# A hybrid HGRN2 and S5 block on one core: half of the S5 setup ordered behind a weight split, later steps of two heads, and the last head's squares on other engines

## The chip, the core and the metric

The kernel runs on one core of a Trainium2 chip. Its engines work from their own in-order queues: TensorE (PE in the profile; its weight loads are PEld), VectorE (DVE), ScalarE (ACT), GpSimd (POOL) and SyncE (SP), which issues DMAs. Engines wait for one another by semaphores, which the tile framework sets from the data that each instruction reads and writes.

The metric is the time of one execution in microseconds on the device, as the median of several runs. Three runs of the kernel before took 796.67, 797.11 and 803.19 us; the median is 797.11 us. One further execution was profiled: it took 799.9 us, of which the profile shows a span of 797.7 us.

## What is computed

One layer of a decoder trunk for 512 tokens of width 1024, in float32, and a final RMSNorm. Cut to what matters here:

```python
h = rmsnorm(x, g)                       # 512 x 1024
q, f, i, og, u, gate_hg, gate_s5 = split(h @ w_in)
# HGRN2, 4 heads of 128, chunks of 64 tokens
f = lb + (1 - lb) * sigmoid(f);  k = 1 - f;  q = silu(q)
b = cumsum(log(f))                      # within a chunk
scores = causal((q * exp(b - b_ref)) @ (k * exp(b_ref - b)).T)
o = scores @ v + (q * exp(b)) @ S_prev  # S: state carried over chunks
o = o * rsqrt(mean(o * o) + eps) * norm_g * silu(og)
# S5, 32 groups with 64 complex states: x_t = A x_{t-1} + B u_t, y = Re(C x) + D u
g = gelu(y);  s5 = g * sigmoid(g @ glu_w + glu_b)
x = x + (sigmoid(gate_hg) * (o @ w_branch_hg) + sigmoid(gate_s5) * (s5 @ w_branch_s5)) @ w_out
x = x + conv_gated_ffn(rmsnorm(x))      # 1024 -> 2 x 2816 -> 1024
x = x + sigmoid(rmsnorm(x) @ w_ple_gate) * (p @ w_ple_proj)
return rmsnorm(x)
```

## The kernel before

**Products in three parts.** Each large float32 operand is split into a high half in a shorter format (float32r) and a low half, the rest. A product is then three matmuls, high x high, high x low and low x high, summed in PSUM (`mm3`, lines 229 to 235; the matmuls are lines 231, 232 and 233 in the profile). The split itself is one copy on ScalarE and one subtraction on VectorE (`split`, lines 241 to 244; the subtraction is line 244).

**Weights** stream through in chunks of up to 128 x 1024. SyncE loads a chunk into `wst` (two slots), ScalarE makes `whi` (three slots) and VectorE `wlo` (three slots), all in `emit_w`. Chunks 0 to 5 hold the weights for u, the input of S5; chunk 6 holds those of f of head 0, chunk 7 q, chunk 8 og. From chunk 3 on the split stands in a block of high priority.

**The order of work.** PE's instructions run in the order in which the program writes them. The main line is: u (`phase_u`, PSUM tiles `psu`, with head 0's f behind it, `pf`), then as `ORDER` says: the rest of head 0, v (`psv`), head 1, gate 0, head 2, gates 1 and 2, head 3, gates 3 to 7, each a run of `mm3`; then the GLU of S5 (`psg`), the two branch products (`pbh`, `pbs`), w_out, the FFN and the last part. Between the `mm3` of the main line stand the small matmuls of the recurrences. They come from two generators, `hg_side` for each head after the other and `s5_side` for four blocks of S5 groups. A counter, `clock`, is raised by 0.65 with each `mm3` and by what a small matmul is put down for; whenever it passes the time that a generator asked for with `yield WAIT[...]`, the next step of that generator is written. `WAIT["hg"][h]` has five entries, the delays ahead of head h's five steps:

- the elementwise work of the head (lines 485 to 517: sigmoids, log, the scan of line 499, the differences of lines 502 and 504, exponentials, products; its last results are `q`, line 513, and `e`, line 511), then entry 0 ahead of the score matmuls `psc`
- entry 1 ahead of the transposes `pk`, entry 2 ahead of the state products `pu`, entry 3 ahead of the outputs `pso`
- then the square of `pso` on ScalarE (line 569), its high and low half on GpSimd (`osh`, line 572, and `osl`, line 573), and entry 4 ahead of the sum over the head, `pms` (lines 576 and 577), and what makes `yhg` of it (lines 579 to 584)

Head h + 1's generator starts when head h's is through. An S5 block makes tables (`Fr`, `Fi`, `Hr`, `Hi`, lines 723 to 742, on VectorE and GpSimd in turn), then the small matmuls `ps5k`, transposes `ps5t` (copied to `et` by ScalarE, line 764), inputs `ps5v`, and, after a scan on VectorE, outputs `ps5y`. When all four are through, `s5_out` brings the result back by DMA (`yT`), applies GELU (`gf`) and splits it (`gh`, `gl`).

The order on VectorE, ScalarE, GpSimd and in the DMA queues is not written by hand. The framework's scheduler takes, by its own estimate of when things are ready, the most urgent instruction that is ready; what was written earlier is more urgent, and a block of high priority more than the rest.

**The S5 setup** (`s5_setup`, lines 615 to 701) is written behind u and in a block of high priority. It works on VectorE in small steps. The first half makes step angles, sine and cosine, the powers `Ar`, `Ai` and the coefficients `nr`, `ni` (to line 685). The second half (from line 686) makes Bbar from them (`bbr`, `bbi`, copied into `Bbr` and `Bbi`) and the powers `Wr`, `Wi` up to 64 by doubling. The reciprocal root of the first norm (`rstd`, lines 344 to 353) and its spreading over the tokens (`dg`, `psR`, `R`, lines 366 to 369) also stand at high priority; `R` scales u (`uT`, line 409), f, q and og (line 480).

**Lines that the steps below touch**: `WAIT` at line 35; `emit_w` with the split in `do`; `split`; in `hg_side` lines 569 to 577; `s5_setup`; the call in the main program behind `phase_u()` and `hg_setup()`.

Of the kernel before, what the change touches and what calls it, by code (L numbers as in the profile page):

```python
# [8 lines left out]
F32 = mybir.dt.float32  # L9
# [3 lines left out]
ALU = mybir.AluOpType  # L13
# [9 lines left out]
HEADS = 4  # L23
# [11 lines left out]
WAIT = {  # L35
    "r": [16.5, 17.5],
    "hg": [[19.5, 3.5, 4.5, 5, 7],
           [13.5, 3.5, 5.5, 5, 10],
           [18.0, 4, 4, 5.5, 7.5],
           [22.0, 3.5, 4, 9, 6.5]],  # L40
    "s5": [[20, 0, 2, 13, 0],
           [9, 2, 16.5, 12.5, 4.0],
           [7, 1.5, 5.5, 15, 0],
# [70 lines left out]
def hybrid_kernel(ctx: ExitStack, tc: tile.TileContext, a):  # L114
# [67 lines left out]
    def split_w(i):  # L182
        split_w_.pop(i)()

    early = {}

    def w_chunk(i, off):
        n = chunk_size(plan[i])
# [6 lines left out]
    def emit_w(dst=None):  # L195
        i = wstate["next"]
        n = chunk_size(plan[i])
        off = wstate["off"]
        wst = early.pop(i, None)
        if wst is None:  # L200
            wst = wp.tile([P, CW], F32, tag="wst", bufs=2, name=f"wst{i}")
            nc.sync.dma_start(wst[:, :n], w_chunk(i, off))
        if dst:
            whi, wlo = dst
        else:
            whi = wp.tile([P, CW], F32R, tag="whi", bufs=LOOK + 1, name=f"whi{i}")
            wlo = wp.tile([P, CW], F32R, tag="wlo", bufs=LOOK + 1, name=f"wlo{i}")

        def do():
            split(whi[:, :n], wlo[:, :n], wst[:, :n])  # L210

        if i < 3:
            split_w_[i] = do
        else:
            with tc.high_priority():
                do()
        wstate["off"] += P * n
        wstate["next"] += 1
        return whi, wlo
# [21 lines left out]
    def split(hi, lo, src):  # L241

        S.activation(hi, src, AF.Copy)  # L243
        V.tensor_tensor(out=lo, in0=src, in1=hi.bitcast(F32), op=ALU.subtract)  # L244

    def act_pair(name):
        return (ap_.tile([P, KD, T], F32R, tag="ahi", name=name + "h"),
# [236 lines left out]
    def hg_side(h):  # L484
# [84 lines left out]
        S.activation(osq, pso, AF.Square)  # L569
        osh = hgt("e1", h, dt=F32R)  # L570
        osl = hgt("e2", h, dt=F32R)
        G.tensor_scalar(out=osh, in0=osq, scalar1=1.0, scalar2=0.0, op0=ALU.mult, op1=ALU.add)
        G.tensor_tensor(out=osl, in0=osq, in1=osh.bitcast(F32), op=ALU.subtract)
        yield WAIT["hg"][h][4]
        pms = small_ps("pms")
        E.matmul(pms, onesr, osh, start=True, stop=False)
# [38 lines left out]
    def s5_setup():  # L615
# [67 lines left out]
        V.tensor_tensor(out=ni, in0=ni, in1=tq, op=ALU.subtract)  # L683
        V.tensor_tensor(out=nr, in0=nr, in1=den, op=ALU.mult)
        V.tensor_tensor(out=ni, in0=ni, in1=den, op=ALU.mult)
        t1, t2 = tmp2(GP, 16)
        cmul(V, br_, bi_, bc(nr.unsqueeze(2), P, GP, 16), bc(ni.unsqueeze(2), P, GP, 16), bcp[:, 0], bcp[:, 1],
             t1, t2)
# [198 lines left out]
    phase_u()  # L887
    hg_setup()
    with tc.high_priority():
        s5_setup()  # L890
    for b in range(4):
        s5_load(b)
    hg = side(hg_all())
# [309 lines left out]
```

## Time and profile before

| what | before |
|---|---|
| median of three runs | 797.11 us |
| the profiled execution's own time | 799.9 us |
| its span in the profile | 797.7 us |
| PE busy | 781.1 us (98%) |
| VectorE busy | 521.3 us (65%) |
| ScalarE busy | 358.2 us (45%) |
| GpSimd busy | 104.7 us (13%) |
| HBM read, written | 80.72 MB, 4.69 MB |

How to read it: a row of the timeline has the start in the span, the duration, the engine, the line, the operation, the tile written and those read, shapes, and in square brackets how long the engine was idle before it and what it waited for. A row of the table of stretches has the stretch, its length, then for each of PE, PEld, DVE, ACT and POOL the busy time and the number of instructions, then the granted TensorE clock as a share of the full one, the mean share of the DMA engines, and GB/s. A row of the view of waits says who waited for whom, how long in total, how often and how long at most. Matmuls are pipelined: one of 128 x 512 is shown with about 0.39 us, while the next may start 0.23 us after it.

### The profile page before, as it was taken

What the parts mean: (1) busy time and instruction counts of PE and PEld (TensorE: products, weight loads), DVE (VectorE), ACT (ScalarE), POOL (GpSimd) and SP (SyncE); (2) the same over time, 40 slices, a digit from 0 to 9 for tenths busy, and PEclk for the clock granted to TensorE, in tenths of its full rate; (3) what the DMA queues carried; (4) which work ended last, traced back from release to release, by engine and by line L of the source; (5) the groups of instructions that cost most, each with busy time, mean ns of one, the idle gap of its engine ahead of it and who ended that gap; (6) DMA issues with size and microseconds to landing.
All of it is one profiled execution on the core that took longest, in us unless ns stands there. A gap on an engine that the chain in (4) does not pass through costs nothing.

```text
span 797.7 us, 9972 instructions
## 1 busy us (share of the span) xinstructions
PE 781.1 (98%) x3806; PEld 640.8 (80%) x3806; DVE 521.3 (65%) x827; ACT 358.2 (45%) x470; POOL 104.7 (13%) x133
## 2 busy tenths in 40 slices
PE   9899999999999999999999999999999999999996
PEld 7687877878888778888888888888888888888885
DVE  7998885898683676375887666777666234144554
ACT  7335373463753933253443443443443133133565
POOL 2044341341521100032000000000000001011000
PEclk9999998999999999999999999999999999999999
DMA  9472524223353232623223233233222223223411
GB/s 336 162 176 79 134 67 109 81 66 110 93 121 95 67 112 99 211 80 106 84 101 106 83 102 106 82 103 106 85 100 93 80 94 105 89 89 138 160 53 53
DMA packets 27039, 86.10 MB, mean 108 GB/s; under 512 B 4720, under 2 KB 4864, under 8 KB 26992
## 3 DMA queue, kind: packets, MB, share of 16 engines
q1 hardware_dynamic: 22608, 77.58, 29.2%
q0 software_dynamic: 3664, 6.84, 4.3%
q10 hardware_dynamic: 720, 1.05, 0.4%
q8 instruction: 30, 0.49, 0.3%
q14 instruction: 17, 0.14, 0.1%
HBM read 80.72 MB, written 4.69 MB: 107 GB/s over the span
## 4 chain that ended last, share of the span: by engine, by line
PE 82%; DVE 9%; issue 2%; DMA 2%; ACT 2%; POOL 1%; SPq 0%; DVEq 0%; POOLq 0%; ACTq 0%
PE pdn L233 5%; PE pdn L232 5%; PE pdn L231 5%; PE puv L231 5%; PE pug L231 5%; PE puv L233 5%; PE pug L233 5%; PE puv L232 5%; PE pug L232 5%; PE pw L233 2%; PE pw L231 2%; PE pw L232 2%; DVE wlo L244 2%; PE ps5y L172 2%; PE pgh L231 1%
## 5 line engine op out<-in xcount | busy, mean ns | idle before, releaser
L243 ACT ACTIVATE whi<-wst 128x1024 fp32r<-128x1024 f32 (+1 forms) x124 | 128.7, 1038 | 269.2 <-issue 77.2
L244 DVE TENSOR_TENSOR wlo<-wst,whi 128x1024 fp32r<-128x1024 f32 (+1 forms) x124 | 153.4, 1237 | 126.0 <-ACT whi L243 126.0
L233 PE MATMUL pdn<-gh,wlo 128*128 128x512 f32 x176 | 70.2, 399 | 0.0
L231 PE MATMUL pdn<-gh,whi 128*128 128x512 f32 x176 | 69.5, 395 | 0.0
L232 PE MATMUL pdn<-gl,whi 128*128 128x512 f32 x176 | 69.4, 394 | 0.0
L231 PE MATMUL pug<-x1gh,whi 128*128 128x512 f32 x160 | 62.2, 389 | 0.0
L232 PE MATMUL pug<-x1gl,whi 128*128 128x512 f32 x160 | 62.2, 389 | 0.0
L233 PE MATMUL pug<-x1gh,wlo 128*128 128x512 f32 x160 | 62.2, 389 | 0.0
L231 PE MATMUL puv<-x1gh,whi 128*128 128x512 f32 x160 | 62.2, 389 | 0.0
L232 PE MATMUL puv<-x1gl,whi 128*128 128x512 f32 x160 | 62.2, 389 | 0.0
L233 PE MATMUL puv<-x1gh,wlo 128*128 128x512 f32 x160 | 62.2, 389 | 0.0
L946 POOL TENSOR_TENSOR sqs<-sqs,sq 128x512 f32<-128x512 f32 x14 | 23.2, 1659 | 222.7 <-ACT sq L945 218.5
L232 PEld LDWEIGHTS pdn<-gl,whi 128*128 128x128 f32 x176 | 33.1, 188 | 8.3
L233 PEld LDWEIGHTS pdn<-gh,wlo 128*128 128x128 f32 x176 | 33.0, 188 | 7.6
L231 PEld LDWEIGHTS pdn<-gh,whi 128*128 128x128 f32 x176 | 33.1, 188 | 7.6
L984 DVE TENSOR_TENSOR u<-pug,R 128x512 f32<-128x512 f32 x20 | 13.8, 692 | 38.4 <-PE pug L233 38.4
L233 PEld LDWEIGHTS puv<-x1gh,wlo 128*128 128x128 f32 x160 | 30.0, 188 | 6.3
L232 PEld LDWEIGHTS pug<-x1gl,whi 128*128 128x128 f32 x160 | 30.0, 188 | 6.3
L233 PEld LDWEIGHTS pug<-x1gh,wlo 128*128 128x128 f32 x160 | 30.0, 188 | 6.3
L232 PEld LDWEIGHTS puv<-x1gl,whi 128*128 128x128 f32 x160 | 30.0, 188 | 6.3
L231 PEld LDWEIGHTS puv<-x1gh,whi 128*128 128x128 f32 x160 | 30.0, 188 | 6.2
L231 PEld LDWEIGHTS pug<-x1gh,whi 128*128 128x128 f32 x160 | 30.0, 188 | 6.1
(398 smaller groups left out, 1823.5 us busy)
## 6 DMA issues: line engine op xcount, KB each, us to landing
wst<-W SPq DMA_DIRECT2D x126, 512.0 KB, 3.3
xt<-x SPq DMA_DIRECT2D x4, 512.0 KB, 9.2
T<-d_k POOLq DMA_DIRECT2D x4, 512.0 KB, 9.4
xr<-xT SPq DMA_DIRECT2D x4, 512.0 KB, 6.5
wst<-W SPq DMA_DIRECT2D x6, 256.0 KB, 2.6
xs<-xT SPq DMA_DIRECT2D x4, 256.0 KB, 4.8
xs<-xT SPq DMA_DIRECT2D x2, 512.0 KB, 7.0
d_u<-uT POOLq DMA_DIRECT2D x4, 256.0 KB, 4.6
```

The lines of the kernel that those rows point to most:

```text
L172: E.matmul(out, w, x, start=start, stop=stop, **kw)
L231: E.matmul(out, wh, xh, start=start, stop=False)
L232: E.matmul(out, wh, xl, start=False, stop=False)
L233: E.matmul(out, wl, xh, start=False, stop=stop)
L243: S.activation(hi, src, AF.Copy)
L244: V.tensor_tensor(out=lo, in0=src, in1=hi.bitcast(F32), op=ALU.subtract)
L946: G.tensor_tensor(out=sqs, in0=sqs, in1=sq, op=ALU.add)
L984: V.tensor_tensor(out=u[:, 2:], in0=ps[i], in1=Rt, op=ALU.mult)
```

## The change

Three things are changed.

- The second half of `s5_setup` becomes a function of its own, `s5_setup2`, and is written with an order edge: each of its VectorE instructions stands behind the VectorE instruction that makes `wlo` of chunk 6 (`lo_ins[6]`, which `split` now returns) in VectorE's queue. The edge sets an order on that queue only; it adds no semaphore. The call is still in the block of high priority.
- Two entries of `WAIT["hg"]`: head 1's entry 0 goes from 13.5 to 16.5, head 3's entry 4 from 6.5 to 8.
- For the last head, the high and low half of the squares are made by `split` (ScalarE and VectorE) and no longer by two GpSimd instructions.

```diff
     "hg": [[19.5, 3.5, 4.5, 5, 7],
-           [13.5, 3.5, 5.5, 5, 10],
+           [16.5, 3.5, 5.5, 5, 10],
            [18.0, 4, 4, 5.5, 7.5],
-           [22.0, 3.5, 4, 9, 6.5]],
+           [22.0, 3.5, 4, 9, 8]],
...
-    early = {}
+    early, lo_ins = {}, {}
...
         def do():
-            split(whi[:, :n], wlo[:, :n], wst[:, :n])
+            lo_ins[i] = split(whi[:, :n], wlo[:, :n], wst[:, :n]).ins
...
         S.activation(hi, src, AF.Copy)
-        V.tensor_tensor(out=lo, in0=src, in1=hi.bitcast(F32), op=ALU.subtract)
+        return V.tensor_tensor(out=lo, in0=src, in1=hi.bitcast(F32), op=ALU.subtract)
...
-        G.tensor_scalar(out=osh, in0=osq, scalar1=1.0, scalar2=0.0, op0=ALU.mult, op1=ALU.add)
-        G.tensor_tensor(out=osl, in0=osq, in1=osh.bitcast(F32), op=ALU.subtract)
+        if h < HEADS - 1:
+            G.tensor_scalar(out=osh, in0=osq, scalar1=1.0, scalar2=0.0, op0=ALU.mult, op1=ALU.add)
+            G.tensor_tensor(out=osl, in0=osq, in1=osh.bitcast(F32), op=ALU.subtract)
+        else:
+            split(osh, osl, osq)
...
         V.tensor_tensor(out=ni, in0=ni, in1=den, op=ALU.mult)
+
+        def rest():
+            with tc.issue_after(lo_ins[6]):
+                s5_setup2(nr, ni, cs, sn)
+        return rest
+
+    def s5_setup2(nr, ni, cs, sn):
         t1, t2 = tmp2(GP, 16)
...
     with tc.high_priority():
-        s5_setup()
+        s5_setup()()
```

## The prediction

> **What bounds the kernel now.** I read the page's first part first: TensorE (PE) is busy for 781.1 of 797.7 us.
>
> ```profile
> span 797.7 us, 9972 instructions
> ...
> PE 781.1 (98%) x3806; PEld 640.8 (80%) x3806; DVE 521.3 (65%) x827; ACT 358.2 (45%) x470; POOL 104.7 (13%) x133
> ```
>
> So a change that takes no work from PE can only win PE's idle time and time at a lowered clock. The view of waits, for PE from 20 to 300 us, lists what PE waited for there (total, times, longest), and the table of stretches gives the granted clock (the third column from the right) of four of them.
>
> ```profile
> PE pf L233 <- DVE wlo L244: 3.4, 1, 3.4
> PE psc L172 <- DVE q L513: 1.4, 1, 1.4
> PE ps5t L763 <- DVE Hi L742: 1.3, 1, 1.3
> PE pms L577 <- POOL e L573: 1.2, 1, 1.2
> PE pms L576 <- POOL e L572: 0.4, 1, 0.4
> PE psc L172 <- DVE d L517: 0.4, 1, 0.4
> ```
>
> ```profile
> 30.00:40.00 10.00, 8.10 (x32) 6.64 (x33) 8.48 (x36) 2.12 (x2) 0.00 (x0) 0.83 0.44 136
> ...
> 70.00:80.00 10.00, 8.70 (x87) 6.81 (x86) 8.04 (x11) 5.24 (x9) 3.06 (x2) 1.00 0.20 61
> ...
> 120.00:140.00 20.00, 19.63 (x135) 15.98 (x133) 9.87 (x21) 6.53 (x9) 2.06 (x3) 0.83 0.43 108
> ...
> 260.00:280.00 20.00, 18.39 (x73) 14.44 (x72) 13.41 (x18) 19.32 (x26) 2.78 (x3) 0.91 0.20 66
> ```
>
> Three places lose time. At 28 us PE waits 3.43 us for the low half of the first head's weights (wlo of chunk 6), and from 30 to 40 the clock is 0.83, which is 10 x 0.17 = 1.7 us more: 5.1 in all. At 118 us it waits 1.42 + 0.37 for head 1's q and its neighbours, and from 120 to 140 the clock is again 0.83: 20 x 0.17 = 3.4, 5.2 in all. At 262 us it waits 0.45 + 1.17 for the last head's squares, and 20 x 0.09 = 1.8 goes with the clock: 3.4 in all. The three edits touch just these places, so the ceiling is 13.7 us. The wait of 1.3 us for Hi at 76 us is followed by a clock of 1.00.
>
> **Edit 1: the second half of the S5 setup behind wlo of chunk 6.** ScalarE finishes whi of that chunk at 25.57 + 1.06 = 26.63; VectorE's queue has by then left the first half of the setup and entered the second, and reaches wlo only at 30.62.
>
> ```profile
> 25.27 0.18 ACT L323 ACTIVATION_READ_ACCUMULATOR xt<-xt 128x1 f32 x1
> 25.57 1.06 ACT L243 ACTIVATE whi<-wst 128x1024 fp32r<-128x1024 f32 x1
> ```
>
> ```profile
> 25.68 0.43 DVE L591 TENSOR_TENSOR tv<-nr,s5p 128x256 f32<-128x256 f32 x1
> 28.58 0.17 DVE L344 TENSOR_SCALAR rs<-ss 128x4 f32<-128x4 f32 x1
> ```
>
> ```profile
> 28.08 0.39 PE L232 MATMUL pf<-xgl,whi 128*128 128x512 f32 x1
> 31.90 0.50 PE L233 MATMUL pf<-xgh,wlo 128*128 128x512 f32 x1 [3.43 <-DVE wlo L244]
> ```
>
> PE's matmuls go at a pitch of 0.227 us, so the third of pf was due at 28.31 and came at 31.90. With the second half ordered behind wlo, only the reciprocal-root chain of L344 to L353 can slip in front: its sums end at 25.27 + 0.18 = 25.45, nine dependent steps of 0.17 us like L344 and a little between them take until about 27.3, and wlo, 1.23 us, then ends at about 28.5. PE loses 0.2 to 0.3 us there in place of 3.6, and its clock should stay up.
>
> That does not make it a gain of 5 us, because nothing leaves VectorE's queue. The whole second half (six products for Bbar, four copies, 36 for the powers W) still runs before head 0's q and before the tables that PE takes next:
>
> ```profile
> 30.62 1.23 DVE L244 TENSOR_TENSOR wlo<-wst,whi 128x1024 fp32r<-128x1024 f32 x1
> 39.71 1.23 DVE L244 TENSOR_TENSOR wlo<-wst,whi 128x1024 fp32r<-128x1024 f32 x1 [1.35 <-ACT whi L243]
> 57.82 4.98 DVE L504 TENSOR_TENSOR f<-b 128x512 f32<-128x512 f32 x1
> 64.84 0.69 DVE L510 TENSOR_TENSOR f<-f,kk 128x512 f32<-128x512 f32 x1 [0.90 <-ACT f L505]
> ```
>
> ```profile
> 71.43 0.68 DVE L513 TENSOR_TENSOR q<-q,b 128x512 f32<-128x512 f32 x1
> 76.81 0.69 DVE L742 TENSOR_TENSOR Hi<-tv,tv 128x512 f32<-128x512 f32 x1 [0.95 <-POOL tv L741]
> ```
>
> ```profile
> 25.60:77.50 51.90, 47.24 (x250) 38.23 (x248) 47.18 (x98) 22.41 (x28) 16.98 (x15) 0.97 0.49 123
> ```
>
> ```profile
> 72.30 0.27 PE L172 MATMUL psc<-q,f 128*64 128x64 f32 x1
> ```
>
> From 25.6 to 77.5 VectorE is busy 47.2 of 51.9 us. PE ended psv and started psc at 72.30, when q had been done for about 0.2 us, and then waited 1.3 us for Hi: it was already level with VectorE. Arriving 5 us earlier, it will wait at psc and at ps5t instead. What edit 1 is worth is what it takes from VectorE's 4.7 us of idle time. The 1.35 us before 39.71 goes, since that wait was for PE to free a slot of whi, which now happens earlier. The rows that wait for ScalarE (0.90 at 64.84) and for GpSimd (about 0.95, twice, before Hr and Hi) stay, and so does the 4.98 us of L504, which took 4.3 longer than L513's 0.68 for the same shape: GpSimd ran its own products meanwhile, and it runs them after the change too. Added is about 0.8 us in which the root chain runs alone, without setup work between its steps. I take 1.35 - 0.8 = **0.5 us**. The bounds: 4.1 if all the idle of the four named places went, and -1.7 if PE's new wait puts it at half speed for a stretch that outlasts Hi (the 1.7 of the first row above; up to Hi a slower PE costs nothing). The order issues no DMA and moves none past another; wst of chunk 8, which waits for wlo of chunk 6 to free its slot, goes out 3 us earlier.
>
> **Edit 2: 13.5 to 16.5 in head 1.** PE's order is written out by a counter that adds 0.65 per group of three matmuls, so psc of head 1 moves back by 3.0/0.65, four or five groups. A group takes 0.68 us:
>
> ```profile
> 259.98 0.39 PE L231 MATMUL pgh<-xgh,whi 128*128 128x512 f32 x1
> 260.66 0.39 PE L231 MATMUL pgs<-xgh,whi 128*128 128x512 f32 x1
> ```
>
> That is 2.7 to 3.4 us of projections ahead of psc. Its first matmul waited for q, and the next ones for e, which ended at 120.28:
>
> ```profile
> 119.73 0.33 PE L172 MATMUL psc<-q,f 128*64 128x64 f32 x2 [1.42 <-DVE q L513]
> ```
>
> ```profile
> 119.60 0.68 DVE L511 TENSOR_TENSOR e<-e,kk 128x512 f32<-128x512 f32 x1
> ```
>
> Without waits psc would have started at 119.73 - 1.42 = 118.31. Its two waits together are 1.79 us, so with 2.7 us or more of work in front of it q and e are there. Both ends of the chain hang on pms of head 0, so edit 1 shifts them together. The wait of 1.79 and the low clock behind it go: **5.2 us**. Everything later in the heads' chain (heads 2 and 3 start when the one before is through) moves back by the same 3.0 against the S5 blocks, which stay. VectorE has room: it idled 10.1 of the 20 us from 120 to 140. The lower bound is a new wait. In block 2, psc of head 2 now falls behind ps5v, and those matmuls were 2.1 us of cover for the second copy of et, which ended 0.2 us before its use:
>
> ```profile
> 179.70 0.58 ACT L764 ACTIVATE et<-ps5t 128x512 f32<-128x512 f32 x1
> ```
>
> ```profile
> 178.34 0.27 PE L172 MATMUL psc<-q,f 128*64 128x64 f32 x1
> 180.47 1.15 PE L172 MATMUL ps5v<-uy,et 128*64 128x64 f32 x32
> ```
>
> If that copy stays where it is in ScalarE's queue, PE waits 2.0 us and loses 1.7 to the clock, so 5.2 - 3.7 = 1.5. I take 5.2, because heads move back on ScalarE as well and et then stands ahead of head 2's exponentials.
>
> **Edit 3: the last head.** pms moves back by 3.0 + 1.5 on the counter. Two groups stood behind it before psg, so it now falls behind the last gate, right ahead of psg; pso moves back 3.0 too. Two GpSimd steps (0.62 and 1.58 us) become a copy on ScalarE and a subtraction on VectorE, by their like 0.63 and 0.69.
>
> ```profile
> 260.52 0.60 ACT L569 ACTIVATE kk<-pso 128x512 f32<-128x512 f32 x1
> 265.41 0.63 ACT L243 ACTIVATE gh<-gf 128x512 fp32r<-128x512 f32 x1
> ```
>
> ```profile
> 261.98 1.58 POOL L573 TENSOR_TENSOR e<-kk,e 128x512 fp32r<-128x512 f32 x1
> ```
>
> ```profile
> 266.07 0.69 DVE L244 TENSOR_TENSOR gl<-gf,gh 128x512 fp32r<-128x512 f32 x1 [0.68 <-ACT gh L243]
> ```
>
> ```profile
> 248.51 0.44 PE L172 MATMUL ps5y<-st,Fi 128*128 128x128 f32 x2
> 265.77 0.63 PE L231 MATMUL psg<-gh,whi 128*128 128x512 f32 x1
> 268.98 0.40 PE L231 MATMUL psg<-gh,whi 128*128 128x512 f32 x1
> ```
>
> The square L569 ran at 260.52, long after pso, because it stood behind a GELU that waited for yT. Squares split at once, the sums are ready at about 260.5 + 0.6 + 0.6 + 0.7 = 262.4. From the end of ps5y (248.7) PE took 17.1 us to psg; without the waits (0.6 and 1.4 by the pitch of 0.227) and 0.4 of low clock it takes 14.6, and 0.6 more because pu of this head now falls behind ps5y instead of ahead of it. So PE comes to pms at about 263.4, a microsecond behind the sums: that wait goes. What is late next is psg, at 263.9: its tenth and eleventh matmuls, 2.0 and 2.3 us in, need the last gh and gl. ScalarE's extra copy of 0.63 pushes these from 266.04 and 266.76 to 266.7 and 267.4. A wait of some 1.2 us is left, and the eleventh matmul starts at 267.5, 18.8 us behind ps5y's end; before, it was one pitch behind 268.98, 20.5 us behind. That is 1.7 us, and ps5y itself comes 0.6 earlier for the pu that is no longer ahead of it: **2.3 us**. Bounds: 3.4 if the GELUs come early, 0.6 if the new wait brings a slow stretch (1.7). The normalisation behind pms stays covered: 48 matmuls of psg and nine of pbh, 13 us, stand before its first use.
>
> **The sum.** 0.5 + 5.2 + 2.3 = 8.0 us. The profiled execution took 799.9 us (797.7 of span and 2.2 around it), so it becomes 791.9; against the median of 797.11, 2.8 below it, the forecast is **789.1 us**.
>
> The Trainium skill, page "TensorE: Matmul & The Clock Gate", section "Part 1: The HAM clock gate", says that the clock falls to half after at least one idle window of about 3.4 us. By it the 1.79 us at 118 would cost no clock, edit 2 would be worth 1.8 and the time would be 792.5. The trace speaks against this: 1.79 us at 118 and 1.62 at 262 were each followed by a low clock, 1.3 at 76 was not. I give it 0.03.
>
> **Rivals.** First, *the whole of the first stall is won*: if head 0's chain and the tables move up in VectorE's queue past the setup and GpSimd's products hit nothing, edit 1 gives 5.1 - 0.3 = 4.8, and 4.8 + 5.2 + 2.3 = 12.3 makes 784.8. For it: L504 alone holds 4.3 us of blocking. Against: the 47.2 us of work would have to end 4.8 us sooner with 4.7 us of idle time in all. Chance 0.13. Second, *the wait moves to ps5v of block 2*: 8.0 - 3.7 = 4.3, 792.8; for it the margin of 0.2 us. Chance 0.20. Third, *the wait moves to psg with a low clock*: 8.0 - 1.7 = 6.3, 790.8. Chance 0.12. Fourth, *wlo does not move up*, because the scheduler fills the place with other urgent work: edit 1 is 0, 789.6, counted with the forecast. Fifth, on the other side, *VectorE runs dry*: with the setup's second half behind wlo, the copy of R, the four uT and head 0's products f, q and og come ahead of it, and this in-order queue stands until PE has delivered psR and pog. From 28.6, pf's remaining 22 matmuls and psR take PE to about 34.5, two projections of eight groups to 45.4. VectorE's work ahead of R (two wlo of 1.23 and some 1.5 of small steps) is done by about 32.5, and that ahead of og (another wlo, seven products of 0.7 to 1) by about 42: it stands 2.0 and 3.4 us, Hi moves back by 5.4, and two slow stretches of 1.7 follow: 0.5 - 5.4 - 3.4 + 7.5 = -0.8, 797.9. It decides from 4.6 us of standing on. Against it: the setup keeps its high priority, the others have none. Chance 0.05.
>
> **From this to the numbers.** The forecast has 0.45 (own range 786.5 to 792), the rivals 0.13, 0.20, 0.12 and 0.05, the page's rule 0.03, and 0.02 is for several at once. The range 784.5 to 797 leaves out about 0.15 of this. A change of 1% is about what a measurement of this kernel can tell from none, and that bound, 789.1, cuts the forecast in half: faster 0.23 + 0.13 + 0.02 and a little of the third rival's spread, 0.40; slower 0.05, the fifth rival with a longer stand; the same 0.55.
>
> **What would show it.** PE's wait at pf under 0.5 us and a clock of 1.00 from 30 to 40; a wait of 2 us or more at psc of head 0 or at ps5t with Hi ending between 75 and 77.5; no wait at psc of head 1 and a clock of 1.00 from 120 to 140; no wait at pms, about 1 us at psg. No wait at all between 60 and 80 would refute the bound on VectorE; a wait at ps5v of block 2 would refute the 5.2.

## The result, and the profile after

The changed kernel took 806.94 us (median of 4 runs, 806.26 to 807.85) against 797.88 us for the kernel before beside it on the same chip (4 runs). The ratio is 1.0108, 95% interval 1.0085 to 1.0132: **slower by 1.1%**, where 789.1 us and a range up to 797.0 were forecast. The profiled execution took 806.26 us, 6.4 more than the one of before, while the medians are 9.1 apart: the profiled execution of before was 2.0 us slower than its median, that of the change 0.7 faster. So the two traces account for 6.4 of the 9.1 us.

The page after, first part:

```profile
span 804.5 us, 9981 instructions
...
PE 784.1 (97%) x3806; PEld 640.3 (80%) x3806; DVE 516.3 (64%) x828; ACT 364.3 (45%) x475; POOL 101.0 (13%) x131
```

PE has the same 3806 matmuls. The view of waits after, for PE from 20 to 300 us:

```profile
PE ps5k L759 <- DVE Fi L738: 1.7, 1, 1.7
PE ps5v L172 <- ACT et L774: 1.5, 1, 1.5
PE pbs L231 <- ACT s5oh L243: 1.3, 1, 1.3
PE ps5t L773 <- DVE Hr L749: 1.3, 1, 1.3
PE ps5t L773 <- DVE Hi L752: 1.2, 1, 1.2
PE pk L546 <- DVE f L532: 1.0, 1, 1.0
PE psc L172 <- DVE q L513: 0.9, 1, 0.9
PE pf L233 <- DVE wlo L244: 0.7, 1, 0.7
PE pbs L232 <- DVE s5ol L244: 0.6, 1, 0.6
...
PE pms L579 <- ACT e L243: 0.3, 1, 0.3
```

All three waits of before shrank: 3.4 to 0.7 at pf, 1.6 to 0.5 at pms (one row of it is below those shown), and psc of head 1 no longer waits; the psc row here is head 2's. Hi is waited for as before (1.3). New are the waits for Fi, Hr, et, f, head 2's q and s5oh, and that for s5ol was 0.2. The granted clock (third column from the right) tells the same story: the three stretches that were low before are at 1.00, and it fell at three other places, at 75, 180 and 285 us.

```profile
30.00:40.00 10.00, 10.00 (x49) 8.40 (x49) 9.58 (x29) 2.13 (x2) 0.63 (x1) 1.00 0.64 210
70.00:80.00 10.00, 5.76 (x33) 3.77 (x24) 7.92 (x13) 3.37 (x6) 4.23 (x3) 0.61 0.16 54
80.00:90.00 10.00, 10.00 (x72) 8.16 (x71) 6.04 (x15) 3.47 (x4) 2.05 (x3) 0.88 0.43 111
120.00:140.00 20.00, 18.96 (x145) 15.19 (x144) 11.39 (x21) 8.79 (x14) 2.58 (x4) 1.00 0.52 133
180.00:200.00 20.00, 18.95 (x108) 15.28 (x107) 15.87 (x34) 4.74 (x6) 2.11 (x2) 0.83 0.41 106
260.00:280.00 20.00, 19.02 (x87) 14.85 (x86) 8.50 (x12) 18.11 (x22) 0.58 (x1) 1.00 0.28 83
280.00:300.00 20.00, 17.71 (x67) 12.69 (x66) 15.78 (x22) 9.86 (x14) 0.00 (x0) 0.91 0.25 80
```

Before, the stretches that fell had a clock of 1.00 (the row for 70 to 80 us stands in the prediction):

```profile
80.00:90.00 10.00, 10.00 (x77) 8.31 (x76) 6.45 (x18) 3.47 (x4) 2.05 (x3) 1.00 0.48 134
180.00:200.00 20.00, 20.00 (x147) 17.36 (x145) 16.39 (x34) 7.42 (x10) 4.34 (x5) 1.00 0.41 113
280.00:300.00 20.00, 19.77 (x86) 15.78 (x85) 14.31 (x20) 6.04 (x8) 0.00 (x0) 1.00 0.38 126
```

**Where the time went.** The main line has the same matmuls in the same order in every kernel here, so each can be looked up in two traces and its start compared. The table gives start after minus start before, in us, for the last main-line matmul that the kernel before starts ahead of 36, 100, 117, 123, 175, 205, 262, 268.3, 283 and 300 us. Negative is a lead over before.

| kernel | 36 | 100 | 117 | 123 | 175 | 205 | 262 | 268 | 283 | 300 |
|---|---|---|---|---|---|---|---|---|---|---|
| the change | -4.3 | +2.0 | +2.0 | -2.9 | -1.8 | +3.9 | +3.9 | +1.3 | +6.2 | +6.8 |
| e1_setup_only | -4.8 | +2.3 | +2.3 | +2.3 | +2.3 | +3.1 | +3.1 | +1.1 | +2.6 | +2.6 |
| e2_head1_only | -0.8 | -1.8 | -1.8 | -6.6 | -5.7 | +0.8 | +0.8 | -1.1 | +1.9 | +1.5 |
| e3_last_only | -1.5 | -1.4 | -1.4 | -0.9 | -1.5 | -1.5 | -1.5 | -5.2 | -0.1 | +1.0 |
| e8_heads_later | 0.0 | -1.4 | -1.4 | -6.2 | -5.2 | -5.0 | -4.5 | -7.7 | -3.4 | -1.7 |
| e9_block0_alone | -3.9 | -4.0 | -4.0 | -1.4 | -1.6 | -1.6 | -1.6 | -3.6 | -2.0 | -2.0 |
| e10_setup_heads | -3.3 | -3.7 | -3.7 | -8.5 | -7.5 | -7.4 | -5.8 | -8.9 | -5.2 | -4.8 |

The first line is the result in short: **PE gets ahead where each edit aims, and each time more is lost at the next place where PE needs something from another engine.** 4.3 us are won at 28 us and 6.3 lost around 75; 4.9 won at head 1 and 5.7 lost at head 2; 2.6 won at the last head and 5.5 lost at pbs.

Each line compares two single executions, and one execution differs from the next. Up to 100 us e2 and e3 have the same matmuls in the same places as before, and yet they are 0.8 and 1.5 us ahead at 36, and 1.8 and 1.4 at 100. Less than 2 us in one column is therefore no proof of an effect. The last pair of numbers needs this most: e1 and e9, which have nothing of the third edit, also win 2.0 us between 262 and 268 and lose 1.5 and 1.6 of it by 283. Before's profiled execution ran at half clock from 264.8 to 268.2 us, and theirs did not. So some 2 of the 2.6 us won there are not the third edit's.

A second account: the waits of PE from 20 to 300 us added up, and what the clock cost there, as the sum over stretches of 5 us of 5 x (1 - granted clock). Before: 8.3 of waits and 6.8 of clock, 15.1. After: 11.6 and 10.2, 21.8. The difference, 6.7, is the difference of the spans (804.5 - 797.7 = 6.8). From 300 us up to PE's last matmul neither has a wait or a low clock. In the other kernels without added matmuls the same account, taken to 300 us, leaves up to 2.3 us open.

*At block 0 of S5* the rows of VectorE show why nothing was kept. Head 0's q ended at 66.0 instead of 72.1, but Hi at 77.6, as before (77.5), and VectorE was busy for 47.6 of the 52.0 us up to there (before: 47.2 of 51.9):

```profile
64.39 1.64 DVE L513 TENSOR_TENSOR q<-q,b 128x512 f32<-128x512 f32 x1 [1.19 <-POOL e L512]
...
71.14 0.76 DVE L738 SCALAR_TENSOR_TENSOR Fi<-tv,tv 128x576 f32<-128x576 f32 x1 [1.05 <-POOL tv L737]
...
76.90 0.69 DVE L752 TENSOR_TENSOR Hi<-tv,tv 128x512 f32<-128x512 f32 x1 [0.95 <-POOL tv L751]
```

```profile
25.60:77.60 52.00, 47.14 (x250) 37.50 (x248) 47.56 (x104) 23.89 (x29) 17.93 (x15) 0.95 0.53 133
```

PE came to psc at 67.80 without a wait, then stood for Fi, Hr and Hi, and left Hi's transposes at half clock (a pitch of 0.43 us in place of 0.23).

*At head 2* the second copy of et stands on ScalarE behind three of head 2's exponentials, and q of head 2 ends at 181.7, 3.5 us later than before (178.2):

```profile
176.19 0.63 ACT L505 ACTIVATE f<-f 128x512 f32<-128x512 f32 x1
176.73 1.04 ACT L243 ACTIVATE whi<-wst 128x1024 fp32r<-128x1024 f32 x1
177.68 0.61 ACT L506 ACTIVATE b<-b 128x512 f32<-128x512 f32 x1
178.20 0.61 ACT L507 ACTIVATE e<-e 128x512 f32<-128x512 f32 x1
178.72 0.58 ACT L774 ACTIVATE et<-ps5t 128x512 f32<-128x512 f32 x1
```

```profile
180.97 0.69 DVE L513 TENSOR_TENSOR q<-q,b 128x512 f32<-128x512 f32 x1
```

Before:

```profile
177.48 0.68 DVE L513 TENSOR_TENSOR q<-q,b 128x512 f32<-128x512 f32 x1
```

*At the tail* ScalarE runs the last head's Ln, the last gate's sigmoid, the head's Exp and the GLU's sigmoids, each with its table load, and the GLU's first sigmoid starts at 279.15 (273.73 before, with three loads, since Ln and Exp stood ahead of both kinds of sigmoid):

```profile
271.53 1.28 ACT L583 ACT_TABLE_LOAD   x1
...
273.54 1.28 ACT L888 ACT_TABLE_LOAD   x1
274.83 1.06 ACT L888 ACTIVATE sig<-sig 128x1024 f32<-128x1024 f32 x1
275.91 1.28 ACT L584 ACT_TABLE_LOAD   x1
...
277.85 1.28 ACT L866 ACT_TABLE_LOAD   x1
279.15 0.69 ACT L866 ACTIVATE sg<-psg,sm 128x512 f32<-128x512 f32 x1
```

### The profile page after: what moved, and what is told of

It reads as the page before. It is cut to its first block, busy times and chain, and to the rows that moved or that the text cites. A ratio compares the mean times of both kernels' runs of the same rounds, so it can differ in the third digit from the quotient of the medians.

```text
span 804.5 us, 9981 instructions
## 1 busy us (share of the span) xinstructions
PE 784.1 (97%) x3806; PEld 640.3 (80%) x3806; DVE 516.3 (64%) x828; ACT 364.3 (45%) x475; POOL 101.0 (13%) x131
## 4 chain that ended last, share of the span: by engine, by line
PE 72%; ACT 3%; DVE 1%; issue 1%; DMA 1%; ACTq 0%; DVEq 0%
PE pdn L233 5%; PE pdn L232 5%; PE pdn L231 5%; PE puv L232 5%; PE pug L232 5%; PE pug L233 5%; PE puv L233 5%; PE puv L231 5%; PE pug L231 5%; PE pw L233 2%; PE pw L231 2%; PE pw L232 2%; PE pbs L232 1%; PE pgs L231 1%; PE pbs L231 1%
## 5 line engine op out<-in xcount | busy, mean ns | idle before, releaser
L244 DVE TENSOR_TENSOR wlo<-wst,whi 128x1024 fp32r<-128x1024 f32 (+1 forms) x124 | 151.0, 1218 | 126.0 <-ACT whi L243 125.9
```

The lines of the kernel that those rows point to most:

```text
L244: return V.tensor_tensor(out=lo, in0=src, in1=hi.bitcast(F32), op=ALU.subtract)
```

## The experiments

**Theory.** An edit that lets PE run early is worth nothing unless the result that PE needs next comes early too; otherwise the lead becomes a wait there, and if the clock falls behind that wait, a loss. **Rival.** One of the edits costs by itself (the added copies on ScalarE, an order on VectorE), and the others are harmless.

### The three edits one by one

`e1_setup_only`, `e2_head1_only` and `e3_last_only` are the kernel before with one edit each. `e4_all_heads_back` is the changed kernel with one number more, so that heads 2 and 3 stand where they stood before:

```diff
-           [16.5, 3.5, 5.5, 5, 10],
+           [16.5, 3.5, 5.5, 5, 7],
```

> The first edit alone: the second half of the S5 setup behind wlo of chunk 6; counter entries and the last head's squares as before. Theory, early PE pays with its clock: Hi still ends at about 77.6 us, PE comes 4.5 us early, waits some 4 us at ps5k and ps5t, and the slow clock that follows outlasts Hi, so PE is 2 us behind the kernel before at 80 us; psc of head 1 waits as before, so the whole is 2 us slower, about 800. Rival, the edit is harmless (the prediction's +0.5) and the loss comes from the later head steps alone: 797 to 798, PE level with before at 80 us.

> The kernel before with one number changed, head 1's entry 0 from 13.5 to 16.5. Theory, later heads' steps pushed into new waits: 5.2 us are won at psc of head 1 (no wait, clock 1.00 from 120 to 140), and lost again: a wait at ps5v of block 2 and a slow stretch near 180 us (some 5 us), and a late last head that delays the GLU's results, with PE waiting at pbs: 797 to 803. Rival, those waits need PE's new lead from the other edits: a clean gain of 5, about 793.

> The last head's part alone: its squares split by ScalarE and VectorE, its last entry 6.5 to 8; setup and head 1 as before. Theory, with pso where it was before this part gains: no wait at pms, a small one at psg, 794.5 to 797, and no wait over 0.5 us at pbs. Rival, the ScalarE queue (gelu, splits, Ln and Exp with their table loads) is what the edit overfills: PE waits at pbs by 1 us or more here too, 798 to 801.

> The changed kernel with one number more: head 1's last entry 7 in place of 10, so pms of head 1 and all of heads 2 and 3 return to about where they stood before, while psc of head 1 keeps its later place. Theory: the waits at ps5v of block 2, psc of head 2 and pbs and the two slow stretches behind them (11 us together) go, what stays is +2 from the setup, -5 at head 1 and -1 to -2 at the last head: 792 to 796. Rival, the waits come from PE's lead and not from the later heads: they stay, 801 to 807.

| kernel | us (median) | ratio to before (95%) |
|---|---|---|
| e1_setup_only | 801.58 | 1.0041 (1.0021 to 1.0060) |
| e2_head1_only | 803.41 | 1.0063 (1.0042 to 1.0084) |
| e3_last_only | 800.50 | 1.0032 (1.0015 to 1.0049) |
| e4_all_heads_back | 804.54 | 1.0083 (1.0056 to 1.0109) |

Before took 798.67 us beside them; the quotients of the medians differ from the ratios by up to 0.1%. Each edit alone came out slower, by 2.9, 4.7 and 1.8 us. For the first two that is clear. The third is not: `e7_last_urgent` below has the same instructions in the same order on every engine as e3, and its ratio is 1.0002 where e3 has 1.0032. Ratios of one and the same order of work, measured at two times, can thus lie 0.3% apart, and every ratio here has to be read with that. The rival falls all the same, since more than one edit costs. e1 and e2 went as their theories say (e2 ended 0.4 us above its range); e3 gave its rival's result. The rows of the three show the same pattern of a lead that turns into a wait. e1, view of waits, with a clock of 0.81 from 60 to 80 us:

```profile
PE ps5k L759 <- DVE Fi L738: 1.7, 1, 1.7
...
PE ps5t L773 <- DVE Hi L752: 1.3, 1, 1.3
...
PE ps5t L773 <- DVE Hr L749: 1.2, 1, 1.2
```
e2, which gains 4.8 us at head 1 (the table above, 117 to 123) with a clock of 1.00, and loses 6.5 at head 2:

```profile
PE ps5v L172 <- ACT et L764: 1.6, 1, 1.6
...
PE psc L172 <- DVE q L513: 0.9, 1, 0.9
```

```profile
120.00:140.00 20.00, 19.06 (x145) 15.52 (x145) 10.69 (x24) 5.72 (x8) 2.06 (x3) 1.00 0.49 119
180.00:200.00 20.00, 20.00 (x109) 16.90 (x110) 14.00 (x29) 4.04 (x5) 1.17 (x1) 0.84 0.25 81
```

e3 has no wait at pms, and is 5.2 us ahead at 268; at 300 it is 1.0 behind. psg waits 0.8 us for gl and pbs 2.5 us for s5ol and s5oh. What pbs needs did not come earlier: the GLU's first sigmoid starts at 273.24, against 273.73 before.

e4 took 804.54 where 792 to 796 had been expected for the case that the later heads are to blame. It has no wait at ps5v, but a longer one at psc of head 2, where PE comes with its lead and q does not:

```profile
PE psc L172 <- DVE q L513: 2.3, 1, 2.3
```

So the place of the later heads is at most a small part of the cause: with them put back the loss is 0.83% in place of 1.08%, each at the edge of the other's interval, and the lead is still lost, one step further on.

### Is it the wait, or the clock behind it?

`e5_fill_waits` and `e15_head1_fill` are e1 and e2 with dummy matmuls in the waits (20 and 13 of them; they feed nothing), so that PE is never idle there.

```diff
+    def fill(b, n, out, w):
+        if b == 0:
+            for _ in range(n):
+                E.matmul(out, onesr, xg[0][:, 0, 0:w], start=True, stop=True)
...
+            fill(b, 8 if i == 0 else 0, pk[:, 0:512], 512)
             E.matmul(pk[i * 32:(i + 1) * 32, 0:P], Bbr[:, b * 4 + i],
...
             pt = small_ps("ps5t")
+            fill(b, (7, 5)[ri], pt, 512)
```

> The setup part alone (as e1_setup_only), with 20 dummy matmuls of 128x512 (about 0.22 us each) put into the waits of TensorE in S5 block 0: 8 ahead of ps5k's matmuls, 7 and 5 ahead of the two groups of ps5t transposes, where e1_setup_only waits 1.7 us for Fi, 1.2 us for Hr and 1.3 us for Hi. They feed nothing. Theory (VectorE's Hi ends no earlier, and the idle time of TensorE brings a slow clock behind it that costs more than the old stall): TensorE is busy instead of idle, the granted clock of 60 to 100 us is 0.95 or more instead of 0.81 and 0.93, the lag behind before at 80 us is 0 to +1 instead of +2.4, and the time is 798 to 800 us, some 2 us under e1_setup_only. Rival (the slow clock comes at these places whatever TensorE does, from its load over a longer time): clock of 60 to 100 us as in e1_setup_only or lower, time 801 to 804 us.

> Head 1's entry alone (as e2_head1_only), with dummy matmuls of 128x512 that feed nothing: 8 ahead of ps5v of block 2 and 5 ahead of psc of head 2, where e2_head1_only waits 1.6 us for et and 0.9 and 0.3 us for q and e, and runs at a clock of 0.84 from 180 to 200 us. Theory (the waits bring the slow clock, and the slow clock is 3 us of the loss): no wait over 0.5 us at these two places, clock of 180 to 200 us 0.95 or more, time 799.5 to 801 us, 2.5 to 4 us under e2_head1_only. Rival (the clock falls there by TensorE's load and not by its waits): clock as before at 0.84, time 803 us or more.

e5 took 799.21 us, ratio 1.0005 (0.9990 to 1.0021), 2.4 under e1; e15 took 800.21, ratio 1.0027 (1.0010 to 1.0045), 3.2 under e2. In e15 the clock is at 1.00 where e2 had 0.84:

```profile
180.00:200.00 20.00, 20.00 (x140) 17.13 (x139) 15.69 (x34) 4.51 (x6) 1.38 (x2) 1.00 0.36 106
```

Nothing that was wanted ran any earlier in these two: Hi ended at 78.6 in e5 and at 77.9 in e1, head 2's q at 179.4 in e15 and at 178.0 in e2. Idle time was only replaced by useless work. So by the medians 2.4 of the 2.9 us of edit 1, and 3.2 of the 4.7 of edit 2, are the **slow clock** behind the new waits. The traces give nearly the same at the places themselves. From Hi's first transpose to pk, with the same 12 matmuls of pf between, PE took 5.4 us in e1 and 3.2 in e5, which is 2.2 less:

```profile
77.99 1.11 PE L773 MATMUL ps5t<-sm,Hi 128*128 128x128 f32 x4 [1.25 <-DVE Hi L752]
...
83.41 0.49 PE L546 MATMUL pk<-sm,f 128*128 128x128 f32 x3
```

```profile
79.14 0.60 PE L780 MATMUL ps5t<-sm,Hi 128*128 128x128 f32 x4
...
82.33 0.49 PE L546 MATMUL pk<-sm,f 128*128 128x128 f32 x3
```

Between 123 and 205 us e2 falls back by 7.4 us against before and e15 by 4.3, which is 3.1 less. In e5 one slow stretch was left, and it lay in the fill itself: the eight dummies ahead of ps5k took 3.64 us, half speed, behind 0.68 us of waiting for e and the small matmuls of psc.

```profile
70.95 3.64 PE L726 MATMUL ps5k<-xgh,onesr 128*128 128x512 f32 x8
75.90 1.79 PE L726 MATMUL ps5t<-xgh,onesr 128*128 128x512 f32 x7
```

### Room in front of the steps

If the leads are lost because PE stands in front of a late result, putting main-line work there should keep them. `e8_heads_later` is e2 with later places for head 2, S5 block 2's states and head 3; `e6_block0_later` and `e9_block0_alone` are e1 with head 0's and block 0's small matmuls 5 to 6 groups of three matmuls later.

```diff
e8  -           [13.5, 3.5, 5.5, 5, 10],      +           [16.5, 3.5, 5.5, 5, 7],
    -           [18.0, 4, 4, 5.5, 7.5],       +           [23.0, 4, 4, 5.5, 4.5],
    -           [22.0, 3.5, 4, 9, 6.5]],      +           [20.0, 3.5, 4, 9, 6.5]],
    -           [7, 1.5, 5.5, 15, 0],         +           [7, 1.5, 8.5, 12, 0],
e6  -    "hg": [[19.5, 3.5, 4.5, 5, 7],       +    "hg": [[24, 3, 3.5, 4, 6],
    -    "s5": [[20, 0, 2, 13, 0],            +    "s5": [[25, 0, 2, 9, 0],
e9  -    "hg": [[19.5, 3.5, 4.5, 5, 7],       +    "hg": [[24, 3, 3.5, 4, 6.5],
    -    "s5": [[20, 0, 2, 13, 0],            +    "s5": [[25, 0, 2, 9.7, 0],
```

> The setup part alone, with head 0's steps put 4.5 groups and S5 block 0's steps 5 groups later in the queue (their last entries shortened by about as much), so that TensorE has some 5 us of projections left to do when it would otherwise stand at ps5k and ps5t of block 0. Theory (the 4.5 us won by the earlier lo half are lost only because TensorE then stands in front of Fi, Hr and Hi, which VectorE finishes at 77.5 us either way): the three waits fall under 1 us together, the granted clock of 60 to 100 us is near 1.00, TensorE is 4 to 5 us ahead of before at 100 us, and unless a later wait takes it the time is 794 to 796 us. Rival (the next result that VectorE delivers, q or f of head 1 or kt of block 0, comes no earlier either): the lead is gone by 140 us in waits of psc or pk of head 1, time 798 to 801 us.

> Before, with head 1's entry of 16.5 as in the change, and the steps of head 2, of S5 block 2's states and of head 3 put 3 groups or more later, so that TensorE has work in front of them when it arrives early. Theory (the 5.2 us won at head 1 are lost because et of block 2 and q of head 2 come no earlier): at ps5v of block 2 and psc of head 2 waits under 0.5 us, clock of 180 to 200 us near 1.00, TensorE still 4 to 5 us ahead of before at 200 us, and 792 to 795 us if the tail lets it through. Rival (the lead is taken by the next place, head 3 or the GLU, where ScalarE's and VectorE's results are no earlier): lead of 4 us or more at 200 us, under 1 us at 290 us, in waits of psc h3, pms, psg or pbs, time 797 us or more.

> The setup part with head 0's and S5 block 0's steps 5 to 6 groups later, as e6_block0_later, but with the entries behind them chosen so that every step from ps5y of block 0 on stands in its old place in the queue of TensorE (in e6_block0_later they stood one group early, and two evictions of the gates fell behind head 3's work on VectorE, 5.3 us of wait). Theory (a lead is kept only where the step that it meets has room): 4 to 5 us ahead of before from 100 to 175 us as in e6_block0_later, then lost at ps5v of block 2 and psc of head 2, which had 0.2 us of margin; time 797 to 800 us, with no wait of 4 us or more at pgh or psg. Rival (head 2's q and block 2's et move with TensorE, because what feeds them is TensorE's own output): the lead is kept to 260 us, time 793 to 796 us.

**e8** took 797.08 us, ratio 0.9981 (0.9962 to 1.0000), 6.3 under e2. The lead of head 1 is now carried to 262 us (-6.2 at 123, -4.5 at 262) with the clock at 1.00 from 100 to 260; then the 7.7 us of 268 become 1.7 at 300, in waits at pbs of 1.8 us for s5ol and 0.6 for s5oh and a low clock. The theory's 792 to 795 had the middle right and the tail too kind; the time is the rival's (797 or more).

**e6** took 809.48 us, ratio 1.0129: a miss, and no test of what it was meant for. Up to 175 us it did as expected (4.6 us ahead at 117, 4.7 at 175, clock of 60 to 100 at 1.00), but for a wait of 1.5 us for Hi. But the shorter delays had put most later steps one group earlier than before. In the order that came of it VectorE took head 3's scan and products ahead of the four multiplications that free two gates' PSUM tiles, and ScalarE's gh was late at psg:

```profile
PE pgh L231 <- DVE sig L887: 5.3, 1, 5.3
PE psg L231 <- ACT gh L243: 4.8, 1, 4.8
```

**e9** repairs that (every step from ps5y of block 0 on in its old place, but for head 0's pms, which stands one group later) and took 798.73 us, ratio 1.0002 (0.9991 to 1.0013), 2.9 under e1. Its lead of 4.0 was expected to last to head 2; it was lost at head 1 instead, the very place that edit 2 gives room to:

```profile
PE psc L172 <- DVE q L513: 2.8, 1, 2.8
...
PE psc L172 <- DVE d L517: 1.5, 1, 1.5
```

The two waits are one stand of PE, behind q and what VectorE makes next, and the clock of 120 to 140 us was 0.84.

### The last head in parts

`e7_last_urgent` is e3 with high priority for the last head's Ln and Exp; `e11_sig_after` is e3 with the last gate's sigmoid behind that Exp on ScalarE; `e13_split_only` is before with the split on ScalarE and VectorE alone, `e14_entry_only` before with the entry of 8 alone.

```diff
e11 +    finish(hg)
    +    with tc.issue_after(exps[3]):
    +        S.activation(sig[7], sig[7], AF.Sigmoid)
    +    s5_glu()
```

> The last head's part alone (as e3_last_only), with the Ln and Exp of the last head's normalisation ahead of the other work in ScalarE's order, so that they run without the sigmoids of another table between them. Theory (in e3_last_only ScalarE is busy without a break from 257 to 278 us, with four table loads of 1.3 us, and the GLU's first sigmoid at 273.2 us is late for TensorE's pbs): one or two table loads fewer, first GLU sigmoid 1.3 to 2.5 us earlier, the pbs waits (2.5 us in all) shrink under 1 us, clock of 280 to 300 us near 1.00, time 796 to 798 us. Rival (pbs waits for a chain through VectorE and DVE's s5ol, not for ScalarE's order): first sigmoid earlier or not, pbs waits over 2 us, time 800 to 801 us.

> The last head's part alone (as e3_last_only), with the last gate's sigmoid put behind the normalisation's Exp on ScalarE, so that it shares the table of the GLU's sigmoids: three table loads instead of four between 265 and 274 us, 1.3 us less, and the sigmoid's 1.06 us no longer between Ln and Exp. (The priority tried in e7_last_urgent left this order as it was.) Theory (ScalarE's queue makes the GLU's first sigmoid late, and pbs waits for it): first GLU sigmoid at or before 272.2 us instead of 273.2 us, pbs and psg waits under 2.5 us in all instead of 3.3 us, time 797 to 799 us. Rival (the waits at pbs come from VectorE's s5ol, whose order is fixed): waits as in e3_last_only, time 800 to 801 us.

> Before, with the last head's squares split by ScalarE and VectorE, all places in TensorE's queue as before. Theory (the copy on ScalarE stands in a queue that is busy from 257 to 278 us, in front of the GELUs' and the GLU's work, and that costs more than the wait at pms that it saves): the wait at pms falls from 1.6 us to under 0.8 us, waits at psg and pbs grow to 2 to 3 us, time 799 to 800.5 us. Rival (the split is a gain, and the later entry is what costs): 796 to 797.5 us.

> Before, with head 3's last entry at 8 and nothing else: pms stands two groups later, right ahead of psg. Theory: the wait at pms goes from 1.6 us to 0.3 us or less, Ln comes later by up to 1.3 us on ScalarE, and so does the GLU's first sigmoid; waits at psg and pbs take what pms gave, time 797.5 to 799.5 us, no difference that can be told. Rival (the later entry alone makes the tail late): 800 us or more.

| kernel | us (median) | before | ratio to before (95%) |
|---|---|---|---|
| e7_last_urgent | 799.10 | 798.69 | 1.0002 (0.9987 to 1.0016) |
| e11_sig_after | 799.30 | 798.57 | 1.0010 (0.9993 to 1.0027) |
| e13_split_only | 798.82 | 798.10 | 1.0004 (0.9985 to 1.0023) |
| e14_entry_only | 798.90 | 798.10 | 1.0012 (0.9994 to 1.0030) |

e7 left ScalarE's order at the tail as it was in e3 (Ln at 266.94, sigmoid, Exp at 271.31, GLU at 273.26), so it tests nothing and is in effect a second e3; that it came out 1.4 us lower, in runs at another time, says how little 1.4 us means here (one execution of before can differ by more, 795.25 to 801.09 us beside e13). e11 did change the order, and the fourth table load is gone: Ln's load, Exp's (268.25) and one for both kinds of sigmoid (270.20) are left. Yet the GLU's first sigmoid started only 0.26 us sooner (272.98; 0.9 us sooner if counted from the load for Ln), and the waits at psg and pbs add up to 2.7 us in place of 3.3. Neither half of the edit alone, nor e11, can be told from no change. The waits at pbs say a little more. They come to 2.4 or 2.5 us in e3, e7 and e14, where the gate's sigmoid stands between Ln and Exp and there are four loads; to 1.9 in e11 and e13, where it stands behind them and there are three; and to 1.5 to 1.9 in e1, e5 and e9, which have nothing of this edit. So about 0.6 us at pbs go with that order on ScalarE, and the rest is there without the edit as soon as PE comes early. What can be said of edit 3: no gain is shown, its loss is between 0 and 0.5%, and the lead of 4 to 5 us that PE has at 268 in e3 (some 2 of it before's slow stretch) is gone by 283, at pbs. Which part of the loss is the split's and which the entry's stays open.

### Everything with room

`e10_setup_heads` is edits 1 and 2 with the room of e8 and e9 (and 12.5 for 12 in block 2); `e12_all_roomy` adds edit 3 and the order of e11; `e16_block0_more` is e12 with block 0 another 3 to 5 groups later (`[25, 3, 3, 3.5, 4.5]` and `[28, 0, 1, 7, 0]`).

> The setup part and head 1's entry of 16.5 together, with room everywhere in front of them: head 0 and block 0 as in e9_block0_alone, heads 2 and 3 and block 2's states as in e8_heads_later. The last head's squares stay on GpSimd. Theory (both gains are real and add up, 4.5 us and 5.2 us, once no step behind them meets a result that comes at its old time): 8 to 10 us ahead of before at 260 us, the granted clock 0.97 or more from 40 to 260 us, then 3 to 4 us lost at pbs as in e8_heads_later: 790 to 793 us. Rival (VectorE, busy 0.8 to 0.9 of 100 to 200 us, cannot deliver 10 us earlier): the lead stops growing at about 6 us, waits for q, f or d of 3 us or more between 120 and 240 us, time 794 to 798 us.

> All three edits, with the room of e10_setup_heads in front of the steps and the sigmoid order of e11_sig_after at the tail. Theory: the lead of e10_setup_heads at 260 us, of which 2 us less is lost at the tail: 788 to 791 us, 1.0 to 1.4 per cent below before. Rival (the tail takes the lead whatever the order, since sg, s5oh and s5ol start only when psg does): 2 us or more above that, 792 to 796 us.

> As e12_all_roomy, with block 0's small matmuls 3 to 5 groups later still, every step from ps5y of block 0 on in the place that it has there. Theory (what is left at block 0 is a matter of room): the waits of 1.7 and 0.7 us at ps5t go under 0.5 us in all, clock 1.00 from 60 to 140 us, and 792 to 794.5 us. Rival (ps5y of block 0 or pms of head 0, whose inputs now come later, take the wait): 794.5 to 797 us with a wait of 1 us or more at ps5y or pms of head 0.

| kernel | us (median) | ratio to before (95%) | waits + clock, 20 to 300 us |
|---|---|---|---|
| e10_setup_heads | 796.48 | 0.9978 (0.9964 to 0.9992) | 6.1 + 1.7 |
| e12_all_roomy | 795.04 | 0.9956 (0.9941 to 0.9970) | 6.4 + 3.4 |
| e16_block0_more | 796.23 | 0.9981 (0.9966 to 0.9996) | 5.8 + 1.7 |

All three came out faster than before, by 0.2 to 0.4%, which for e10 and e16 is no more than e3 and e7 lie apart, and by 10 to 12 us faster than the change. None is as fast as expected (790 to 793, 788 to 791, 792 to 794.5). **The leads do add up where there is room**: e10 is 8.5 us ahead at 123 and 7.4 at 205. Then it loses 1.6 by 262 and some 4 at pbs, as e8 does. e16 did away with the waits at ps5t and got another in their place, 1.9 us at pk of head 0 for VectorE's f, with a clock of 0.83 from 80 to 90:

```profile
PE pk L546 <- DVE f L532: 1.9, 1, 1.9
```

That is the rival's answer, one step away from where it was looked for. e12, at 795.04, has the lowest median measured here; its interval overlaps e10's.

## Why the prediction was wrong

**Edit 1.** Right: wlo of chunk 6 at 27.74 (ending 29.0; about 28.5 was forecast), 0.7 us of wait at pf (0.2 to 0.3), clock 1.00 from 30 to 40, and Hi at 77.6, no earlier. VectorE does bound this stretch. The 4.98 us of L504 did not stay, but moved: L504 took 0.68 us, and L594 (3.19) and L513 (1.64) were slow instead, beside GpSimd's products. Half wrong: the place (psc found q ready; the waits are at ps5k, and at ps5t as forecast). Wrong, and the step that failed: the term. The 0.5 us stood on "up to Hi a slower PE costs nothing", and the case that the slow stretch outlasts Hi was a bound, -1.7. It was the outcome: three waits of 1.7, 1.3 and 1.2 us followed one another, the clock was 0.5 from 72 to 82, and the edit cost 2.9 us (e1), of which e5 gives back 2.4. In this order of work the old stall, 3.6 us at 28, had cost next to nothing, since PE was level with VectorE at 72 anyway: without it, and with the waits filled, e5 is at 1.0005.

**Edit 2.** The 5.2 us are there: no wait at psc of head 1, clock 1.00 from 120 to 140, a lead that grows by 4.9 us. The step that failed is the choice "I take 5.2, because heads move back on ScalarE as well and et then stands ahead of head 2's exponentials". It stood behind three of them. The rival at this place had chance 0.20 and a price of 3.7 (2.0 of wait and 1.7 of clock); it did happen, and the price was higher, since head 2's own q is late too (0.9 and 0.2 us) and the clock cost 3.4: 5.7 us between 175 and 205, 6.5 in e2. Also wrong: "everything later in the heads' chain moves back by the same 3.0". psc of head 2 stands 2 groups later, its pms 5, psc of head 3 stands 6 and its pso 9, because a step begins where the counter next passes its time.

**Edit 3.** The wait at pms fell to 0.5 us, and about 0.4 came at psg in place of 1.2. Up to psg the gain is 2.6 us in the change (3.9 to 1.3 in the table); that this is near the forecast 2.3 is luck, since e1 and e9 win 2.0 there without the edit. The step that failed is the one that looks behind pms, "the normalisation behind pms stays covered", and stops there. yhg was indeed not waited for, but nothing in the working asked when pbs gets s5oh and s5ol, which came no earlier: that is where the lead went (2.2 us of waits and 1.7 of clock in the change). That the table loads for Ln and Exp, ahead of the GLU's sigmoids on ScalarE, are the reason is shown for about 0.6 us only.

**The sum** took each removed wait, with its slow clock, as a gain to the end. Margins of the next meeting point were looked up only at psc of head 0 and at ps5v (0.2 us each), and at ps5v the lead was credited all the same. The fifth rival had the right sign and the wrong place. The range ended at 797.0 because the bounds were too kind: the lower ones of the three edits, -1.7, 1.5 and 0.6, still add up to a gain of 0.4 us, 796.7, while the edits alone measured losses of 2.9, 4.7 and, less surely, 1.8.

**The prices of the clock** were those of one execution. The 1.7, 3.4 and 1.8 us of low clock that the sum wins back are what before's profiled execution happened to pay. With the same waits at the same places e3 paid nothing behind pf, e7, e11 and e14 paid 1.7 behind head 1's psc, and e1, e5 and e9, with 1.2 us at pms, paid nothing there.

## What to carry to other kernels

A wait that is removed on the engine that sets the end is worth the margin of the next few results it needs from elsewhere, not its own length: list for each following meeting point when the other engine delivers, and credit only what those allow. Move the consumers, too: some 2 to 10 groups of independent work in front of the next late results turned a loss of 1.1% into a gain of 0.4% (in e12, with one sigmoid moved, whose own part is not shown). Afterwards compare the starts of the same instructions in the two traces, which shows in one line where a gain was made and where it was given back, and put a kernel without the edit beside them, to see what one execution alone does.

## What the runs showed of the hardware

The clock's cost came in portions. From 20 to 300 us the sums over stretches were 1.7, 3.4, 5.1 or 5.2, 6.8, 8.6, 10.2 and 11.9 us over the 18 kernels profiled, that is one to seven times 1.7, and a low stretch ran at 0.50 (2 us stretches of e2 from 180 to 186 are all at 0.50). 1.7 us is what 3.4 us at half speed cost. One and the same wait did not always bring the same number of portions. Head 1's 1.4 and 0.4 us at psc brought two in before, e1, e3, e5 and e13, and one in e7, e11 and e14. The wait at pf, 2.8 to 3.8 us, brought none in e3, two in e14, and one in before, e2, e7, e8, e11, e13 and e15. 1.7 us at pbs brought one in e12 and e13 and none in e5, e11 and e16.

The Trainium skill, page "TensorE: Matmul & The Clock Gate", section "Part 1: The HAM clock gate", has a table of two states, half and full clock, and a free-running window of about 3.4 us. The trace agrees with the two states and with that length, but not with the same table's condition for the low state, an idle window of that length: waits of 1.5 and 0.9 us with 1.6 us of work between them brought it at head 2, and 0.7 us for e followed by the small matmuls of psc did in e5. The length of a wait alone does not decide here. That it is where the wait falls in such a window would fit the numbers of portions above, but was not tried.

ScalarE had four table loads of 1.28 us between 271 and 279 us in the change, one each for the Ln and the Exp of one normalisation. In e11 these two stand next to each other, and both still load.
